# Two-layer decoder trunk on one core: retention scores of both heads in turn, regrouped retention outputs, and the first down-projection operands prepared and evicted on VectorE

## The chip, the cores and the metric

The kernel runs on one core of one Trainium2 chip. A core has TensorE (matrix products; the profile calls its products PE and its weight loads PEld), VectorE (DVE), ScalarE (ACT), GpSimd (POOL) and the queue of SyncE (SP) that issues the transfers. The metric is the device time of one execution, in microseconds (us); lower is better.

## The reference, cut to what matters

Each of two layers normalizes the 1024 x 1024 input, projects it into twelve slices of 256 columns, feeds four groups (a 31-tap convolution module, stick-breaking attention, chunkwise retention, a short gated convolution), projects their concatenation back, and then runs a gated convolutional feed-forward block. The change touches retention and the start of the feed-forward block's last product. Retention, for four heads of 64 columns and eight chunks of 128 positions:

```python
    def step(state, inp):
        qc, kc, vc = inp
        inner = jnp.einsum('bhqd,bhkd->bhqk', qc, kc) * d_intra
        o = jnp.einsum('bhqk,bhkd->bhqd', inner, vc) + jnp.einsum('bhqd,bhde->bhqe', qc, state) * q_decay[..., None]
        state = state * chunk_decay[:, None, None] + jnp.einsum('bhkd,bhke->bhde', kc * k_decay[..., None], vc)
        return state, o
...
def conv_ffn(x, w_up, w_conv, w_down):
    h = causal_dwconv(x @ w_up, w_conv)
    gate, up = jnp.split(h, 2, axis=-1)
    return (jax.nn.silu(gate) * up) @ w_down
```

## The kernel before

All large products are made in three passes: every operand is split into a rounded high part and a low part (`split`, L180 to L182: a ScalarE copy for the high part, then a VectorE subtraction for the low part), and high x high, high x low and low x high are added up in PSUM.

**The mixer of a layer.** Twenty-four column blocks of the input projection are computed one after another (`project`, L210, products of 128 x 128 by 512 columns). Between the eight inner steps of each block a slot counter advances (`run_slot`, L590), and each slot runs what is due in it: attention score units, retention steps, and the taps of the 31-tap convolution (L261, VectorE), which are put behind other work by a low priority. TensorE's order in this region is exactly the order of the program text; the other engines' orders are set by priorities. Retention runs twice per layer, for head pair 0 (from slot 94) and head pair 1 (from slot 160); its steps come at the offsets in `RET_AT`, 0, 6, 9, 12, 14, 17 and 18 for the part that matters here:

- offset 0: products for the states (L465 to L467), then the state recurrence on VectorE (L474 to L479);
- offsets 6 and 9: the scores of head 0 over all eight chunks, then of head 1 (L490 to L492, 24 products each). The two heads of a pair lie in the lower and upper 64 rows of the key tiles kh and kl and of the query tiles q2, so each product uses 64 of the 128 rows. `bank()` gives the PSUM tile. VectorE masks the result (L494), and `split` makes the high and low halves `it`;
- offsets 12, 14, 17, 18: the outputs, for each head and each half of four chunks (L510 and L512). For each chunk there is one product over all 128 rows (values with `it`), and, except for the very first chunk, one over the head's 64 rows (state with query), added to the same place. ScalarE and VectorE evict the result (L514 to L516).

**The feed-forward block.** The last gate and up products (`ffn_products`, L894) leave TensorE through the PSUM tiles x, y and z; the last eviction of x is the copy L948 on ScalarE. The down projection then takes over the same PSUM space (L1050). Its 22 column blocks are added up in ten chunks; for each chunk and each of eight row blocks `down_tok` (L982) makes 12 products (L977) into one of three rotating PSUM tiles. In the first chunk the result is copied to an SBUF tile by ScalarE (L987), in later chunks it is added by VectorE (L989). The operands of block j, the weights and the gated activations gd, come through `down_split` (L958): a transfer into a raw tile (L961), a ScalarE cast for the high part (L966), a subtraction for the low part (L967, on GpSimd or VectorE), and only then is the raw tile free again. Blocks 0 to 3 are loaded while the last `ffn_products` is still running (`freed`, L1028).

## Time and profile before

| what | value |
|---|---|
| median of three runs | 2420.81 us (2415.92 to 2422.47) |
| the profiled execution | 2420.78 us, of which its span is 2419.0 us |
| PE, PEld busy | 2329.3 us (96%), 1901.0 us (79%) |
| DVE, ACT, POOL busy | 1652.4 us (68%), 1094.2 us (45%), 239.4 us (10%) |
| mean granted TensorE clock | 0.985 |

A share of busy time is an average over stages. TensorE is busy nearly everywhere, and the change is worth what it is worth in the few stretches that it touches, so those are what the rows below are taken from. In a timeline row the bracket holds the idle time before the instruction and what ended it. In the chain of waits a step's length is the time from the end of the step before, so for products that follow each other it is the pace, while a timeline row's own length includes the overlap with its neighbours.

### The profile page before, as it was taken

How to read it: one execution, taken by the hardware profiler on the slowest of the kernel's cores; microseconds unless marked ns; L12 is line 12 of the kernel's file. 1: busy time of each engine (PE TensorE's matmuls, PEld its weight loads, DVE VectorE, ACT ScalarE, POOL GpSimd, SP SyncE). 2: the span in 40 equal slices, each digit the busy share in tenths (PEclk: the TensorE clock that was granted, in tenths of full speed). 3: DMA queues.
4: the chain of work that ended last, by engine and by line, in shares of the span. 5: the costliest groups of instructions: out<-in, count | busy, mean ns of one | idle time of the engine just before them, and what ended most of it. 6: DMA issues, size and time to landing. Idle time of an engine off the chain costs nothing.

```text
span 2419.0 us, 26348 instructions
## 1 busy us (share of the span) xinstructions
PE 2329.3 (96%) x10596; PEld 1901.0 (79%) x10596; DVE 1652.4 (68%) x1717; ACT 1094.2 (45%) x1479; POOL 239.4 (10%) x100
## 2 busy tenths in 40 slices
PE   7998999999999999999999989999999999989998
PEld 6877787777888887888778767878888888877886
DVE  4699875549777777344557997765597777763445
ACT  5653564434444455421347535653345544453102
POOL 0000000000000002743210000000000000045420
PEclk9998999999999999999999989999999999999999
DMA  4212212412222224422222122123122222224223
GB/s 148 70 53 62 61 36 71 146 54 87 70 88 87 79 79 148 175 86 88 96 70 70 53 62 54 34 96 131 53 87 79 86 89 88 79 104 174 87 70 122
DMA packets 58811, 209.88 MB, mean 87 GB/s; under 512 B 7104, under 2 KB 7872, under 8 KB 58688
## 3 DMA queue, kind: packets, MB, share of 16 engines
q1 hardware_dynamic: 58688, 208.19, 26.0%
q8 instruction: 83, 1.36, 0.2%
q14 instruction: 40, 0.33, 0.0%
HBM read 159.93 MB, written 39.85 MB: 83 GB/s over the span
## 4 chain that ended last, share of the span: by engine, by line
PE 37%; DVE 7%; ACT 3%; DMA 2%; issue 1%; POOL 0%; DVEq 0%; SPq 0%; POOLq 0%; ACTq 0%
PE pp L210 10%; PE pp L977 9%; PE ppx L894 8%; PE ppy L894 4%; DVE u L261 2%; PE ppz L894 2%; PE pp L731 1%; DVE u L182 1%; ACT u L151 1%; PE op L409 1%; DVE u L379 1%; DVE u L167 1%; DMA u<-gd 0%; PE tp L396 0%; DMA wr<-in_w_out 0%
## 5 line engine op out<-in xcount | busy, mean ns | idle before, releaser
L261 DVE SCALAR_TENSOR_TENSOR u<-u,par,u 128x1023 f32<-128x1023 f32 (+10 forms) x280 | 363.8, 1310 | 45.2 <-ACT u L786 40.9
L989 DVE TENSOR_TENSOR u<-u,pp 128x1024 f32<-128x1024 f32 x143 | 174.5, 1221 | 234.7 <-PE pp L977 234.6
L210 PE MATMUL pp<-hH,wh 128*128 128x512 f32 x960 | 327.0, 411 | 0.7 <-DVE u L182 0.5
L210 PE MATMUL pp<-hL,wh 128*128 128x512 f32 x960 | 313.0, 397 | 0.0
L967 POOL TENSOR_TENSOR u<-u,u 128x1024 fp32r<-128x1024 f32 x48 | 119.6, 2507 | 1937.9 <-DVE u L940 1853.0
L210 PE MATMUL pp<-hH,wl 128*128 128x512 f32 x960 | 311.1, 395 | 0.0
L977 PE MATMUL pp<-u,u 128*128 128x512 f32 x1152 | 268.9, 394 | 14.3 <-ACT u L948 8.5
L977 PEld LDWEIGHTS pp<-u,u 128*128 128x128 f32 x1152 | 217.4, 190 | 62.8 <-ACT u L948 9.4
L210 PEld LDWEIGHTS pp<-hL,wh 128*128 128x128 f32 x960 | 183.5, 191 | 40.4
L210 PEld LDWEIGHTS pp<-hH,wl 128*128 128x128 f32 x960 | 183.1, 191 | 40.5
L210 PEld LDWEIGHTS pp<-hH,wh 128*128 128x128 f32 x960 | 172.2, 192 | 37.0 <-issue 5.5
L731 PE MATMUL pp<-u,hH 128*128 128x512 f32 x512 | 140.2, 392 | 0.2
L977 PE MATMUL pp<-hH 128*128 128x512 f32 x576 | 131.5, 389 | 0.0
L977 PEld LDWEIGHTS pp<-hH 128*128 128x128 f32 x576 | 108.1, 188 | 22.4
L786 ACT ACTIVATE u<-u,par 128x1024 f32<-128x1024 f32 x76 | 87.7, 1155 | 73.7 <-DVE u L940 66.5
L894 PE MATMUL ppx<-u,wh 128*128 128x512 f32 x384 | 118.7, 390 | 1.8 <-ACT u L935 1.5
L966 ACT CAST u<-u 128x1024 fp32r<-128x1024 f32 x48 | 50.2, 1052 | 136.7 <-DMA u<-in_w_down 87.8
L731 PEld LDWEIGHTS pp<-u,hH 128*128 128x128 f32 x512 | 95.0, 188 | 20.2 <-ACT u L181 1.0
L195 DVE TENSOR_TENSOR wl<-wr,wh 128x1024 fp32r<-128x1024 f32 x60 | 73.6, 1227 | 51.6 <-ACT wh L193 51.4
L894 PE MATMUL ppx<-u,hH 128*128 128x512 f32 x352 | 108.4, 389 | 0.0
L193 ACT CAST wh<-wr 128x1024 fp32r<-128x1024 f32 x60 | 62.9, 1049 | 70.9 <-PE pp L210 56.3
L379 DVE TENSOR_TENSOR_SCAN u<-pp,u 128x1023 f32<-128x1023 f32 (+3 forms) x64 | 87.7, 1401 | 0.7
(243 smaller groups left out, 4457.2 us busy)
## 6 DMA issues: line engine op xcount, KB each, us to landing
wr<-in_w_up SPq DMA_DIRECT2D x50, 512.0 KB, 3.5
wr<-in_w_in SPq DMA_DIRECT2D x48, 512.0 KB, 3.6
gd<-u SPq DMA_DIRECT2D x44, 512.0 KB, 2.9
u<-in_w_down SPq DMA_DIRECT2D x44, 512.0 KB, 4.8
u<-gd SPq DMA_DIRECT2D x44, 512.0 KB, 4.1
u<-in_w_up SPq DMA_DIRECT2D x38, 512.0 KB, 4.3
xs<-u SPq DMA_DIRECT2D x24, 512.0 KB, 2.6
u<-xs SPq DMA_DIRECT2D x24, 512.0 KB, 3.6
```

Of the source, the lines that this page charges most:

```text
L193: nc.scalar.copy(wh, raw)
L195: eng.tensor_sub(wl, raw, wh.bitcast(F32))
L210: nc.tensor.matmul(ps[:, half * 512:(half + 1) * 512], w[:, kt, :], m[:, 4 * half:4 * half + 4, kt, :], start=(kt == 0 and m is hH and w i ...
L261: eng.scalar_tensor_tensor(acc[:, lo:hi], src[:, lo - s:hi - s], wc, acc[:, lo:hi], ALU.mult, ALU.add)
L379: nc.vector.tensor_tensor_scan(rev, z[:, o + 1:e + 1][:, ::-1], rev, r[:, e:e + 1], ALU.add, ALU.add)
L731: nc.tensor.matmul(ps[:, hs], a[:, t, k, :], w[:, hs], start=(k == 0 and a is hH and w is wo[k][0]), stop=(k == KT - 1 and a is hL))
L786: nc.scalar.activation(acc, ps, AF.Copy, scale=par[:, w + 2:w + 3])
L894: nc.tensor.matmul(ps, a[:, kt, :], x(m, kt), start=start and kt == 0 and a is wh and m == 0, stop=kt == 3 and a is wl, skip_group_check=True)
L966: nc.scalar.copy(h, raw)
L967: (nc.gpsimd if n is not None or len(slot_of) % 2 else nc.vector).tensor_sub(lo, raw, h.bitcast(F32))
L977: nc.tensor.matmul(ps[:, hs], a[:, ts_], w[:, hs], start=(i == 0 and w is h and a is gh), stop=(i == len(gs) - 1 and a is gl))
L989: nc.vector.tensor_add(facc[t], facc[t], ps)
```

## The change

The change has four parts.

1. The two score steps no longer belong to one head each. Each now covers one half of the chunks (four of eight) and both heads, and the products alternate between head 0 (lower 64 rows) and head 1 (upper 64 rows). Within one PSUM tile the two heads lie in different banks.
2. An output group issues its four 128-row products first and its three or four 64-row products after them, instead of in turn.
3. In `down_split`, the subtraction for the first four blocks of a layer (eight tiles) is on VectorE; for all later ones on GpSimd. Before, the tiles of those first blocks went to GpSimd or VectorE by the parity of the number of tiles in use.
4. The eviction of the first chunk in `down_tok` is on VectorE, with a raised priority, instead of on ScalarE.

```diff
@@ retention
-        its = []
-        for hh in range(2):
-            rows = slice(HD * hh, HD * hh + HD)
-            ip = ptile(bank(), (P, NB, P))
-            for c in range(NB):
+        its = [[], []]
+        for half in range(2):
+
+            ip = ptile(bank(), (P, 2, 4, P))
+            for j in range(4):
+                c = 4 * half + j
                 cs = slice(c * P, (c + 1) * P)
-                nc.tensor.matmul(ip[:, c, :], kh[rows, cs], q2[c // 4][rows, c % 4, 0], start=True, stop=False)
-                nc.tensor.matmul(ip[:, c, :], kh[rows, cs], q2[c // 4][rows, c % 4, 1], start=False, stop=False)
-                nc.tensor.matmul(ip[:, c, :], kl[rows, cs], q2[c // 4][rows, c % 4, 0], start=False, stop=True)
-            m = ualloc(F32, (P, NB, P))
-            nc.vector.tensor_mul(m, ip, tri.unsqueeze(1).broadcast_to([P, NB, P]))
-            it = [ualloc(F32R, (P, 4, 2, P)) for _ in range(2)]
-            for half in range(2):
-                split(it[half][:, :, 0, :], it[half][:, :, 1, :], m[:, 4 * half:4 * half + 4, :])
+                for a, part in ((kh, 0), (kh, 1), (kl, 0)):
+                    for hh in range(2):
+                        rows = slice(HD * hh, HD * hh + HD)
+                        nc.tensor.matmul(ip[:, hh, j, :], a[rows, cs], q2[half][rows, j, part],
+                                         start=(a is kh and part == 0), stop=(a is kl))
+            m = ualloc(F32, (P, 2, 4, P))
+            nc.vector.tensor_mul(m, ip, tri.unsqueeze(1).unsqueeze(1).broadcast_to([P, 2, 4, P]))
+            for hh in range(2):
+                it = ualloc(F32R, (P, 4, 2, P))
+                split(it[:, :, 0, :], it[:, :, 1, :], m[:, hh])
+                its[hh].append(it)
             ufree(m)
-            its.append(it)
-            if hh == 1:
+            if half == 1:
                 ufree(kh, kl)
             yield
...
                 for j in range(4):
                     c = 4 * half + j
-                    nc.tensor.matmul(op[:, j], value_block(v2, c, hh), it[half][:, j], start=True, stop=(c == 0))
+                    nc.tensor.matmul(op[:, j], value_block(v2, c, hh), it[half][:, j], start=(j % 2 == 0),
+                                     stop=False, skip_group_check=True)
+                for j in range(4):
+                    c = 4 * half + j
                     if c:
-                        nc.tensor.matmul(op[:, j], st[rows, c - 1, :], q2[half][rows, j], start=False, stop=True)
+                        nc.tensor.matmul(op[:, j], st[rows, c - 1, :], q2[half][rows, j], start=False,
+                                         stop=(j % 2 == 1), skip_group_check=True)
@@ down_split
-            (nc.gpsimd if n is not None or len(slot_of) % 2 else nc.vector).tensor_sub(lo, raw, h.bitcast(F32))
+            (nc.gpsimd if len(loads) >= 4 else nc.vector).tensor_sub(lo, raw, h.bitcast(F32))
@@ down_tok
             if first:
                 facc[t] = ualloc()
-                nc.scalar.copy(facc[t], ps)
+                with tc.high_priority(offset=HPE):
+                    nc.vector.tensor_copy(facc[t], ps)
```

Outside the places shown here the engines' orders are the same as before, in particular VectorE's order in the mixer.

The first place is TensorE, the last retention output group of layer 1, head pair 1. In a row the PSUM tile stands left of the arrow, then the moving and the stationary operand: u_696 is `it`, u_682 the values, u_684 the queries, u_688 the states. Before, and after:

```order
L510 MATMUL pp_278_11256<-u_696_11119,u_682_10847 128x256
L512 MATMUL pp_278_11256<-u_684_10865,u_688_10914 128x256
L510 MATMUL pp_278_11256<-u_696_11119,u_682_10847 128x256
L512 MATMUL pp_278_11256<-u_684_10865,u_688_10914 128x256
L510 MATMUL pp_278_11256<-u_696_11119,u_682_10847 128x256
L512 MATMUL pp_278_11256<-u_684_10865,u_688_10914 128x256
```

```order
L513 MATMUL pp_278_11256<-u_696_11121,u_682_10847 128x256 x4
L518 MATMUL pp_278_11256<-u_684_10865,u_688_10914 128x256 x4
```

Eight products that took turns between the two kinds are now two runs of four.

The second place is VectorE at the start of the down projection of layer 1: L930, L936 and L940 evict and add the last gate and up products, L261 are the taps of the last block, L989 is the first addition of the second chunk. Before:

```order
L795 TENSOR_TENSOR u_935_14876<-u_935_14876,u_937_14902 128x1024
L930 TENSOR_TENSOR u_946_14926<-u_944_14924,ppz_350_14923 128x512
L936 TENSOR_TENSOR u_947_14927<-u_945_14925 128x512
L940 TENSOR_TENSOR u_946_14926<-u_944_14924,ppy_349_14922 128x512
L261 SCALAR_TENSOR_TENSOR u_966_15043<-u_946_14926,par,u_966_15043 128x1023
```

After (L937, L943 and L947 are the old L930, L936 and L940; L974 is the moved subtraction, L995 the moved eviction):

```order
L974 TENSOR_TENSOR u_953_14962<-u_951_14959,u_952_14961 128x1024
L937 TENSOR_TENSOR u_946_14926<-u_944_14924,ppz_350_14923 128x512
L974 TENSOR_TENSOR u_959_14987<-u_957_14984,u_958_14986 128x1024
L943 TENSOR_TENSOR u_947_14927<-u_945_14925 128x512
L947 TENSOR_TENSOR u_946_14926<-u_944_14924,ppy_349_14922 128x512
L974 TENSOR_TENSOR u_950_14956<-u_948_14953,u_949_14955 128x1024
L974 TENSOR_TENSOR u_965_15025<-u_963_15022,u_964_15024 128x1024
L261 SCALAR_TENSOR_TENSOR u_966_15043<-u_946_14926,par,u_966_15043 128x1023
L974 TENSOR_TENSOR u_956_14981<-u_954_14978,u_955_14980 128x1024
L261 SCALAR_TENSOR_TENSOR u_966_15043<-u_946_14926,par,u_966_15043 128x1022
L995 COPY u_968_15086<-pp_351_15073 128x1024
```

The subtractions now stand among the evictions of the last products, and the copies of the first chunk follow them on the same engine.

The third place is ScalarE at the same time, between the eviction L935 and the last eviction of the x tile (L948, after the change L955). Before:

```order
L935 COPY u_945_14925<-ppx_348_14921 128x512
L966 CAST u_949_14955<-u_948_14953 128x1024
L966 CAST u_955_14980<-u_954_14978 128x1024
L966 CAST u_964_15024<-u_963_15022 128x1024
L786 ACTIVATE u_966_15043<-u_946_14926,par 128x1024
L948 COPY u_947_14927<-ppx_348_14921 128x512
```

```order
L942 COPY u_945_14925<-ppx_348_14921 128x512
L973 CAST u_949_14955<-u_948_14953 128x1024
L973 CAST u_964_15024<-u_963_15022 128x1024
L793 ACTIVATE u_966_15043<-u_946_14926,par 128x1024
L973 CAST u_955_14980<-u_954_14978 128x1024
L955 COPY u_947_14927<-ppx_348_14921 128x512
```

The same three casts and the same activation stand ahead of that eviction, with one cast now behind the activation.

## Rows read from the trace of the kernel before

**Rows 1.** The page, part 1: busy time, share of the span, instructions.

```profile
PE 2329.3 (96%) x10596; PEld 1901.0 (79%) x10596; DVE 1652.4 (68%) x1717; ACT 1094.2 (45%) x1479; POOL 239.4 (10%) x100
```

**Rows 2.** Busy time by stretch; columns PE, PEld, DVE, ACT, POOL, PEclk, DMA, GB/s.

```profile
262.00:340.00 78.00, 77.85 (x399) 64.25 (x398) 58.72 (x68) 52.31 (x67) 0.00 (x0) 1.00 0.15 41
969.60:973.00 3.40, 3.40 (x10) 2.63 (x8) 1.50 (x1) 2.89 (x3) 3.40 (x2) 0.50 0.00 0
1399.00:1433.40 34.40, 28.80 (x133) 23.08 (x131) 33.64 (x49) 11.08 (x18) 0.00 (x0) 0.90 0.34 92
1570.00:1615.00 45.00, 45.00 (x191) 32.53 (x191) 22.52 (x29) 20.41 (x24) 0.00 (x0) 0.96 0.24 80
```

**Rows 3.** The chain of waits, layer 1 (head pair 1, down projection): start, step, what.

```profile
1563.31 0.95 PE op L409 x8
...
1572.30 0.11 PE pp L491
...
1594.74 0.11 PE pp L510
1594.85 0.31 PE pp L512
...
1596.72 0.31 PE pp L512
...
2195.01 212.51 PE pp L977 x936
```

**Rows 4.** The same chain, layer 1, head pair 0, half clock.

```profile
1410.96 0.21 PE pp L492
...
1433.87 0.51 PE pp L512
1434.38 0.51 PE pp L510
```

**Rows 5.** What TensorE waited for from 1399 to 1462 us: total, times, longest.

```profile
PE pp L510 <- DVE u L379: 4.3, 1, 4.3
PE pp L510 <- DVE u L516: 3.5, 1, 3.5
```

**Rows 6.** Timelines of VectorE and TensorE, layer 1, head pair 0, first output group.

```profile
1423.40 1.23 DVE L329 SCALAR_TENSOR_TENSOR u<-pp,u 64x1024 fp32r<-64x1024 f32 x1
...
1425.08 0.40 PE L510 MATMUL pp<-u,u 128*128 128x256 f32 x2
```

**Rows 7.** What TensorE waited for from 940 to 1005 us (layer 0).

```profile
PE pp L977 <- ACT u L948: 3.3, 1, 3.3
PE pp L977 <- ACT u L987: 0.5, 1, 0.5
```

**Rows 8.** The same from 2130 to 2205 us (layer 1).

```profile
PE pp L977 <- ACT u L948: 5.2, 1, 5.2
PE pp L977 <- ACT u L987: 3.8, 3, 1.5
```

**Rows 9.** Timelines of ScalarE, GpSimd and VectorE, start of layer 1's down projection.

```profile
2154.34 1.05 ACT L966 CAST u<-u 128x1024 fp32r<-128x1024 f32 x1 [6.36 <-DMA u<-gd]
...
2160.64 1.99 ACT L966 CAST u<-u 128x1024 fp32r<-128x1024 f32 x2 [3.83 <-POOL u L967]
...
2163.59 0.56 ACT L948 COPY u<-ppx 128x512 f32<-128x512 f32 x1
...
2155.46 5.15 POOL L967 TENSOR_TENSOR u<-u,u 128x1024 fp32r<-128x1024 f32 x2 [5.33 <-ACT u L966]
...
2155.90 2.50 DVE L936 TENSOR_TENSOR u<-u 128x512 f32<-128x512 f32 x1 [5.70 <-ACT u L935]
2158.32 0.68 DVE L940 TENSOR_TENSOR u<-u,ppy 128x512 f32<-128x512 f32 x1
```

**Rows 10.** The page, part 5: a VectorE and a GpSimd subtraction; idle time before them.

```profile
L967 POOL TENSOR_TENSOR u<-u,u 128x1024 fp32r<-128x1024 f32 x48 | 119.6, 2507 | 1937.9 <-DVE u L940 1853.0
...
L195 DVE TENSOR_TENSOR wl<-wr,wh 128x1024 fp32r<-128x1024 f32 x60 | 73.6, 1227 | 51.6 <-ACT wh L193 51.4
```

## The prediction

> **What bounds the kernel now.** The page comes first: TensorE is busy for 2329.3 of 2419.0 us, no other engine for more than 68% [rows 1]. A shorter product therefore shortens the kernel, but only where TensorE is not already waiting, so I read each stretch that the change touches by itself [rows 2]. During the second retention pass of a layer (head pair 1, 1570 to 1615 us in layer 1) TensorE is busy for 45.00 of 45.00 us and VectorE for half of that: here a saved TensorE microsecond is a saved microsecond. During the first half of head pair 0 (1399 to 1433 us) it is the other way round: VectorE works for 33.64 of 34.40 us, and TensorE has 5.6 us to spare. From 262 to 340 us in layer 0, after head pair 0, TensorE is busy for 77.85 of 78.00 us again. Then I read what TensorE waits for. In head pair 0 it waits twice for VectorE before output products, 3.5 and 4.3 us [rows 5]. At the start of the down projection it waits for ScalarE: 3.3 + 0.5 us in layer 0 [rows 7], 5.2 + 3.8 us in layer 1 [rows 8]. Last, the pace of products that follow each other, as steps of the chain [rows 3].
>
> **Part 2, the regrouped outputs.** Eight attention products of one shape (128 rows, 256 columns) take 0.95 us, 0.12 each. In an output group the same size takes 0.11 for the first product and then 0.31 at every further step, because each one goes from 128 rows to 64 or back [rows 3]. So a change of shape costs 0.31 - 0.12 = 0.19 us. A group of eight has seven such changes inside, a group of seven (first half, no state for chunk 0) five; the return to the projection comes on top both times. After the change each has one. That saves 6 x 0.19 = 1.15 and 4 x 0.19 = 0.76 us. One head pair has two groups of each kind: 3.8 us. At head pair 1 all of it lies on TensorE's path: 2 layers x 3.8 = **7.6 us**.
>
> At head pair 0 the first group is worth nothing. It starts at 1425.08, right behind a VectorE eviction (L329) that runs from 1423.40 to 1424.63 [rows 6] in a queue without a gap, and the group behind it waits 3.5 us for L516 of the same queue. From that group on VectorE waits for TensorE's outputs, and a shorter group is passed on. These groups run mostly at half the granted clock, where a change of shape makes a step 0.51 us against 0.21 for a step that stays in one shape [rows 4] (the 0.21 is a score product's): 6 x 0.30 = 1.8 for the second group, 4 x 0.30 = 1.2 for the third, and 1.15 (layer 0, full clock) or 1.8 for the fourth. That is 4.15 + 4.8 = 8.95 us in the two layers. I keep two thirds, **6 us**, because the wait of 4.3 us for L379 moves only as far as its own chain through ScalarE and VectorE does; the bounds are 2.4 (only the last group counts, at full clock) and 9.
>
> **Part 1, the scores.** A score product takes a step of 0.11 us [rows 3], 24 make 2.7 us. The multiplications and splits on VectorE and ScalarE keep their number, size and place. No row shows two heads alternating, so the step is bounded from both sides. If the products of the two heads run beside each other, 24 take 12 steps, 1.35 us less. If each has to wait for the other as now, nothing is saved. If going from the lower to the upper 64 rows costs what a change of shape costs, each takes 0.31 and a group loses 24 x 0.2 = 4.8 us. I take a gain of 1.2: both heads use products of the same shape, so the nearest row is the step that stays in one shape, not the one that changes it, and the two heads have different rows and different PSUM banks. At head pair 1 that is 2 groups x 2 layers x 1.2 = **4.8 us**. At head pair 0 it is nothing: the queue that has no gap there is VectorE's.
>
> The Trainium skill's page "TensorEngine Tiling (Array Packing)", section "Key Properties", says that only changing the tiling mode drains the engine and that different tiles load weights and multiply in parallel; by it the gain is 1.35 per group, 5.4 us in all, and the sum would be 0.6 us lower. No row of before shows it.
>
> **Parts 3 and 4, the start of the down projection.** In layer 1, TensorE's first down product waits 5.2 us for the eviction L948, which ScalarE starts at 2163.59 and ends at 2164.15 [rows 8, 9]; so the gate and up products were over at 2158.95. Ahead of L948 in ScalarE's queue stand casts that wait until 2160.64 for GpSimd, which works off two subtractions in 5.15 us [rows 9]. On VectorE a subtraction takes 1.23 instead of 2.51 us [rows 10], and its neighbours lose a brake: the 512-column addition L936 took 2.50 us beside a busy GpSimd, L940 of the same width 0.68 [rows 9]. With a subtraction ahead of them (its cast ends at 2155.4, so until 2156.6), L936 and L940 end near 2158.0 instead of 2159.0. Then ScalarE has an activation (the 0.96 us between its casts' end and L948), a cast of 1.05 and L948 itself with 0.56: 2160.6. The wait falls from 5.2 to 1.7: 3.5 us. In layer 0, with 3.3 us of wait and the same queue, I take 2.3. The copies L987 (0.5 + 3.8 us of waits) leave a queue of casts that wait for transfers; VectorE needs 1.2 us for each and a row block takes 12 products of 0.227 (212.51 us for 936 [rows 3]), 2.7 us, so with three PSUM tiles they are covered even behind one tap and one subtraction: 4.3 us gone. Together 10.1 us; the bounds are 4.3 - 2 = 2 (the eviction as late as now, some copies late) and 12.8 (all waits gone). The wait in layer 0 is followed by 3.4 us of half clock with ten products, where 15 would fit [rows 2]: 1.1 us. If that goes in both layers it is 2.2 more; I count 0.7 and keep the rest for the range. The sum for these parts is **10.8 us**.
>
> What is queued behind the moved work: VectorE's taps of the last block, which nobody on TensorE needs before the last chunk. GpSimd loses 16 of its subtractions and is not waited for later.
>
> **The sum.** 7.6 + 6 + 4.8 + 10.8 = 29.2 us. The profiled execution took 2420.8 (2419.0 of span and 1.8 around it), the same as the median, so the forecast is 2391.6, **2392 us**. Its own range is 2384 to 2400.
>
> **Rivals.**
> *Loads one after another.* The score step of 0.11 us is as long for 128 columns as the 0.12 step for 256 [rows 3]; so it isn't the multiplication that sets it. If it is the weight load and loads never overlap, alternating heads gains nothing: 2391.6 + 4.8 = 2396 us. The Trainium skill's page "TensorE: Matmul & The Clock Gate", section "LDWEIGHTS (loading the stationary operand)", says that a load's time goes by its columns, not its rows, which fits this; the same page lets a load overlap a product of other rows.
> *The wait moves to VectorE.* Subtractions now stand between the evictions L930, L936 and L940 in VectorE's queue. A subtraction waits for its cast, a cast for its transfer, and one cast waited 6.36 us for one [rows 9]. If L940, and behind it L948, come as late as now, only the copies' 4.3 us less a little are saved: 2391.6 + 8 = 2400 us. Against it: that cast ended at 2155.4, early enough.
> *Alternating heads costs, slower.* If going to the other head's rows costs 0.2 us at full clock, as a change of shape does, head pair 1 loses 4 x 4.8 = 19 us and head pair 0, after its 3.8 us of spare time a layer, 2 x (9.6 - 3.8) = 12. Against the other 24.4 us that is about 2427 us, slower than before, and more where the half clock lasts longer. It decides from about 0.17 us per alternation, (24.4 + 7.6) / 192.
>
> **How the numbers follow.** The forecast has 0.66, the loads one after another 0.15, the wait on VectorE 0.12, the costly alternation 0.07 (the shape stays the same, which speaks against it). The first three end more than 0.3% below 2420.8, that is below 2413.5; 0.3% is about what a measurement of this kernel can tell from no change. With small parts of each for something unseen: faster 0.91, within 0.3% 0.04, slower 0.05. The range for 8 in 10 takes in the second and third case and the bounds of head pair 0 and of the half clock: 2383 to 2405 us.
>
> **What would show it.** Score products of head pair 1 at steps near 0.06 (right), 0.11 (rival 1) or 0.3 (rival 3); an output group of eight in about 1.2 us instead of 2.3; head pair 0 with the same end of its first output group as before; TensorE's wait for the eviction after the last gate and up product below 2 us, and no wait for the first chunk's copies. Wrong would be the forecast if TensorE waited longer for VectorE at the scores or outputs of head pair 1, or if VectorE's idle time at the start of the down projection ended on transfers.

## The result, and the profile after

The changed kernel takes 2386.25 us (median of four runs, 2384.02 to 2386.96) beside 2420.36 for the kernel before: a ratio of 0.9862 (95% interval 0.9849 to 0.9875), 34 us less (30 to 37). A second set of runs, the repeat further below, gave 0.9847 (0.9832 to 0.9862). Two executions of the experiments, one of `o_heads` (3838 us) and one of `best` (2566 us), ran at a lower granted clock (0.56 and 0.85) and are left out of the times below. The forecast was 2392, its range 2383 to 2405: right in direction and range, 6 us too high. The profiled execution took 2386.67 us, 2384.9 of it its span.

The page of the changed kernel, part 1, answers to [rows 1]: TensorE is busy for 32.0 us less, GpSimd for 43, VectorE for 22 more.

```profile
PE 2297.3 (96%) x10596; PEld 1885.0 (79%) x10596; DVE 1674.2 (70%) x1749; ACT 1080.7 (45%) x1463; POOL 196.5 (8%) x84
```

In the changed kernel the lines have moved: L494 is every score product, L513 the 128-row and L518 the 64-row output products, L901 the gate and up products, L955 the last eviction of x, L973 and L974 cast and subtraction of `down_split`, L984 the down products, L995 the first chunk's evictions. The chain of waits (start, step, what) at head pair 1 of layer 1 answers to [rows 3]: 24 score products take 1.49 us, 0.062 a step instead of 0.11, and an output group of eight is 0.47 + 0.66 us with one change of shape inside.

```profile
1561.72 1.49 PE pp L494 x24
...
1574.90 0.47 PE pp L513 x4
1575.37 0.66 PE pp L518 x4
```

What TensorE waited for in the whole run (total, times, longest), some rows: the waits of head pair 0 for VectorE (L379, L329, L523) answer to [rows 5]. The kernel before has, in its whole run, 8.6 us for L379 as well and these two:

```profile
PE pp L510 <- DVE u L516: 5.7, 2, 3.5
PE pp L510 <- DVE u L329: 1.1, 1, 1.1
```

In the changed kernel the wait for L379 is as long as before; that for L329, ahead of the first output product, has grown from 1.1 to 7.5 us, since TensorE comes to it earlier, and that for the addition L523 (L516 before) has fallen from 5.7 to 4.9.

```profile
PE pp L513 <- DVE u L379: 8.6, 2, 4.3
PE pp L513 <- DVE u L329: 7.5, 2, 3.8
...
PE ppx L901 <- DVE u L261: 5.7, 1, 5.7
PE pp L513 <- DVE u L523: 4.9, 2, 3.0
PE pp L984 <- ACT u L955: 4.6, 2, 3.0
```

The same view of two stretches, the start of the down projection in layer 0 and in layer 1, answers to [rows 7] and [rows 8]. The copies' waits are gone in both layers; the wait for the last x went from 5.2 to 1.5 us in layer 1 and hardly moved in layer 0.

```profile
PE pp L984 <- ACT u L955: 3.0, 1, 3.0
```

```profile
PE pp L984 <- ACT u L955: 1.5, 1, 1.5
```

Where the time went, from the starts of the same products in the timelines of the two profiled executions (us):

| product | before | after | shift |
|---|---|---|---|
| layer 0: first score product, head pair 0 | 209.41 | 208.13 | -1.3 |
| first score product, head pair 1 | 371.02 | 366.56 | -4.5 |
| product behind the last output group | 407.89 | 396.79 | -11.1 |
| first gate and up product of the last stage | 599.24 | 588.96 | -10.3 |
| last gate and up product ends | 964.80 | 953.73 | -11.1 |
| layer 1: first score product, head pair 0 | 1407.77 | 1398.04 | -9.7 |
| first score product, head pair 1 | 1571.97 | 1557.23 | -14.7 |
| product behind the last output group | 1610.40 | 1587.47 | -22.9 |
| last gate and up product ends | 2158.98 | 2134.86 | -24.1 |
| end of the span | 2419.0 | 2384.9 | -34.1 |

The first 1.3 us lie ahead of every changed instruction. Between the end of layer 0's down projection (1222.2 before, 1210.0 after, a shift of -12.2) and layer 1's first score product 2.5 us are lost, where nothing was changed: that much a single trace leaves open. The mean granted clock there (from 973 to 1408 us) is 1.00 before; the changed kernel's trace has two short falls in it, 0.65 from 1217.0 to 1220.5 us and 0.69 from 1326.5 to 1330.0.

### The profile page after: what moved, and what is told of

It reads as the page before. It is cut to its first block, busy times and chain, and to the rows that moved or that the text cites. A ratio compares the mean times of both kernels' runs of the same rounds, so it can differ in the third digit from the quotient of the medians.

```text
span 2384.9 us, 26334 instructions
## 1 busy us (share of the span) xinstructions
PE 2297.3 (96%) x10596; PEld 1885.0 (79%) x10596; DVE 1674.2 (70%) x1749; ACT 1080.7 (45%) x1463; POOL 196.5 (8%) x84
## 4 chain that ended last, share of the span: by engine, by line
PE 38%; DVE 7%; ACT 3%; DMA 1%; issue 1%; DVEq 0%; SPq 0%
PE pp L984 10%; PE pp L210 9%; PE ppx L901 8%; PE ppy L901 4%; DVE u L261 2%; PE ppz L901 2%; PE pp L738 1%; DVE u L182 1%; ACT u L151 1%; DMA wr<-in_w_out 1%; PE op L409 1%; DVE u L379 1%; DVE u L167 1%; PE tp L396 0%; DMA wr<-in_w_up 0%
## 5 line engine op out<-in xcount | busy, mean ns | idle before, releaser
L261 DVE SCALAR_TENSOR_TENSOR u<-u,par,u 128x1023 f32<-128x1023 f32 (+10 forms) x280 | 356.3, 1284 | 28.6 <-ACT u L793 24.4
L984 PE MATMUL pp<-u,u 128*128 128x512 f32 x1152 | 266.0, 392 | 6.1 <-ACT u L955 4.6
L984 PEld LDWEIGHTS pp<-u,u 128*128 128x128 f32 x1152 | 216.6, 189 | 52.4 <-ACT u L955 5.4
L974 POOL TENSOR_TENSOR hH<-u,hH 128x1024 fp32r<-128x1024 f32 x24 | 58.1, 2451 | 1946.5 <-ACT hH L973 1946.5
L984 PE MATMUL pp<-hH 128*128 128x512 f32 x576 | 131.5, 389 | 0.0
L984 PEld LDWEIGHTS pp<-hH 128*128 128x128 f32 x576 | 108.1, 188 | 22.4
L901 PE MATMUL ppx<-u,wh 128*128 128x512 f32 x384 | 118.4, 389 | 0.3 <-ACT u L926 0.3
L973 ACT CAST u<-u 128x1024 fp32r<-128x1024 f32 x48 | 50.2, 1052 | 128.9 <-DMA u<-in_w_down 85.7
L901 PE MATMUL ppx<-u,hH 128*128 128x512 f32 x352 | 108.4, 389 | 0.0
L379 DVE TENSOR_TENSOR_SCAN u<-pp,u 128x1023 f32<-128x1023 f32 (+3 forms) x64 | 87.8, 1403 | 0.7
```

The costliest lines, as they stand in the source:

```text
L261: eng.scalar_tensor_tensor(acc[:, lo:hi], src[:, lo - s:hi - s], wc, acc[:, lo:hi], ALU.mult, ALU.add)
L379: nc.vector.tensor_tensor_scan(rev, z[:, o + 1:e + 1][:, ::-1], rev, r[:, e:e + 1], ALU.add, ALU.add)
L901: nc.tensor.matmul(ps, a[:, kt, :], x(m, kt), start=start and kt == 0 and a is wh and m == 0, stop=kt == 3 and a is wl, skip_group_check=True)
L973: nc.scalar.copy(h, raw)
L974: (nc.gpsimd if len(loads) >= 4 else nc.vector).tensor_sub(lo, raw, h.bitcast(F32))
L984: nc.tensor.matmul(ps[:, hs], a[:, ts_], w[:, hs], start=(i == 0 and w is h and a is gh), stop=(i == len(gs) - 1 and a is gl))
```

## The experiments

**One part at a time.** Each kernel is the kernel before with one or two parts of the change; the diffs are those of the section on the change, so only the part is named.

Part 1 alone.

> The kernel before with part 1 alone (scores of both heads in turn). Theory: a group of 24 score products passes in 1.5 us instead of 2.8, and this counts at head pair 1 alone, where TensorE has no idle time: 4 groups x 1.33 = 5.3 us, so about 2415 beside 2420.4. At head pair 0 the groups get shorter too, but the output products behind them wait the longer for VectorE: nothing. Rival 1: head pair 0 counts as well, 8 x 1.33 = 10.6 us, 2410. Rival 2: the alternation gains only together with part 2: within 1 us of before.

Measured: 2409.9 us, ratio 0.9962 (0.9950 to 0.9974) to 2418.8, so 9.2 us less (6.3 to 12.1). From the first score product of head pair 1 to the product behind its last output group it takes 34.15 us in both layers, the kernel before 36.87 and 38.43. The first difference is 2.7 = 2 x 1.33, as expected; the second has another 1.6 in it, which is half clock (a granted clock of 0.50, the 1.2 GHz level). Rows of the windows view (columns as in [rows 2]) just behind the second score group of head pair 1, of the kernel before and of the changed kernel, show it:

```profile
1580.60:1584.00 3.40, 3.40 (x8) 2.45 (x8) 2.66 (x5) 1.14 (x2) 0.00 (x0) 0.50 0.49 154
```

```profile
1563.20:1566.60 3.40, 3.40 (x13) 2.12 (x12) 2.26 (x3) 2.09 (x3) 0.00 (x0) 1.00 0.03 6
```

TensorE never rested there, yet behind the second group of 24 score products of one head the granted clock fell to 0.50. In the five profiled kernels with the old scores (ten such stretches, two layers each) there are eight such windows, in seven of the ten; in the nine with both heads in one group (eighteen stretches) none. Why the clock falls there is not shown. At head pair 0 the trace gains 1.3 and 2.6 us over the two layers' stretches (first score product of head pair 0 to that of head pair 1), not nothing. But in the four profiled kernels whose code for it is that of before, this stretch takes 161.6 to 163.3 us in layer 0 and 161.8 to 164.2 in layer 1, so a gain of this size is not clear of the difference between executions. The first output product starts where it did, 17.0 us behind the first score product, so what is gained comes later; in layer 1 the mean granted clock of the stretch is 0.94 instead of 0.92, in layer 0 0.94 as before. The wait of the first output product takes the rest; it was 1.1 us in all in the kernel before:

```profile
PE pp L513 <- DVE u L329: 6.3, 2, 3.8
```

Rival 2 is out. By time, the 5.3 us of the theory lie outside the interval and the 10.6 of rival 1 inside it; by the trace part 1 is worth 5.3 us at head pair 1, 1.6 of clock there, and some 2 to 4 at head pair 0.

Part 2 alone.

> The kernel before with part 2 alone (output products regrouped, scores as before). Theory: at head pair 1 a group of eight passes in 1.23 instead of 2.40 us and one of seven in 1.11 instead of 1.88, (1.17 + 0.77) x 2 groups x 2 layers = 7.8 us; at head pair 0 the gain of the first group is lost in a wait for VectorE and the others give about 7: 15 us, so about 2405. Rival: head pair 0 stays with VectorE all the way and gives nothing alone: 7.8 us, about 2413.

Measured: 2408.9 us, ratio 0.9957 (0.9945 to 0.9970), 10.4 us less (7.3 to 13.3), between the two expectations: the interval takes in the rival's 7.8 and not the theory's 15. The groups of head pair 1 are as expected (1.23 and 1.11 us), 7.8 us; but this execution has three windows of half clock behind score groups of head pair 1, the one before had one, and so it loses 3 us of it again. Head pair 0 gains 2.7 and 3.6 us by its stretches. Its waits have grown here too (L520 is the second addition of an output group, L516 in [rows 5], which has 5.7 us in the whole run of before):

```profile
PE pp L510 <- DVE u L520: 8.9, 2, 4.5
```

Parts 3 and 4 together.

> The kernel before with parts 3 and 4 alone (first subtractions and first evictions of the down projection on VectorE). Theory: layer 0 gives 1 us (only the copies' waits), layer 1 about 9 to 10 (3.5 of the wait for the last gate and up eviction, 3.8 of the copies' waits, the rest the half clock that followed): 10 to 11 us, about 2410. Rival: part of this came from parts 1 and 2, since they bring the stage forward against its transfers: then it is under 7 us, over 2413.

Measured: 2403.1 us, ratio 0.9941 (0.9928 to 0.9954), 14.3 us less (11.1 to 17.4). From the last gate and up product to the end, layer 1 gains 7.8 us in the trace (the wait for the last x falls to 2.1, the copies' waits go), and the two gate and up stages are 1.7 us shorter each; 1.5 us of that is a wait for L935 in the kernel before, which is gone. Layer 0 keeps its wait:

```profile
PE pp L977 <- ACT u L948: 2.9, 1, 2.9
```

The three kernels' gains, 9.2 + 10.4 + 14.3, make 33.9 us, and the whole change gives 33 to 37: the parts add up as far as their intervals of about 3 us either way can tell.

**Parts 3 and 4 apart.**

> The kernel before with part 3 alone (the first subtractions on VectorE, the first chunk's copies still on ScalarE). Theory: parts 3 and 4 need each other. The first down product of layer 1 starts 3.5 us earlier, but the copies stay in ScalarE's queue behind casts that wait for transfers, so their wait grows from 3.8 to about 7 us: under 1.5 us in all, 2419 or more. Rival: the parts add up, 3.5 us in layer 1 and about 1 of the half clock behind it: about 2416, with the copies' wait at 3.8 as before.

Measured: 2405.6 us, ratio 0.9950 (0.9938 to 0.9962), 12.1 us less (9.2 to 15.0). My theory fell, and the rival's reason too: the copies, although they are still on ScalarE, no longer keep TensorE waiting in layer 1, and do so for 1.5 us in layer 0. What TensorE waited for there, in layer 1 and in layer 0:

```profile
PE pp L977 <- ACT u L948: 3.9, 1, 3.9
```

```profile
PE pp L977 <- ACT u L948: 2.6, 1, 2.6
PE pp L977 <- ACT u L987: 1.5, 1, 1.5
```

ScalarE's timeline in layer 1, of the kernel before and then of this one, tells why for the first copies. Ahead of them stands the activation L786 of the last block. In the kernel before ScalarE stood idle for 3.73 us ahead of it, until a GpSimd subtraction ended; with VectorE's subtractions that is 0.57.

```profile
2170.82 1.15 ACT L786 ACTIVATE u<-u,par 128x1024 f32<-128x1024 f32 x1 [3.73 <-POOL u L967]
...
2174.23 2.85 ACT L987 COPY u<-pp 128x1024 f32<-128x1024 f32 x3
```

```profile
2162.20 1.15 ACT L786 ACTIVATE u<-u,par 128x1024 f32<-128x1024 f32 x1 [0.57 <-DVE u L967]
2163.25 1.91 ACT L987 COPY u<-pp 128x1024 f32<-128x1024 f32 x2
```

In the kernel before that is 1.0 of the 3.8 us, TensorE's wait at 2175.29. The other two waits, 1.5 us at 2185.26 and 1.3 at 2195.01, are for copies behind casts that wait for transfers, as the prediction said. But GpSimd is behind the first of these too: no transfer was issued between 2155.07 and 2176.49, when a subtraction freed the raw tile, and that one (L967 into hL) stood behind others in GpSimd's queue. TensorE, ScalarE, GpSimd and SyncE (SPq) in the kernel before:

```profile
2175.29 8.48 PE L977 MATMUL pp<-u,u 128*128 128x512 f32 x36 [1.02 <-ACT u L987]
2185.26 5.05 PE L977 MATMUL pp<-u,u 128*128 128x512 f32 x21 [1.49 <-ACT u L987]
...
2183.25 1.05 ACT L966 CAST hH<-u 128x1024 fp32r<-128x1024 f32 x1 [6.17 <-DMA u<-in_w_down]
2184.20 1.00 ACT L987 COPY u<-pp 128x1024 f32<-128x1024 f32 x1
...
2161.77 9.02 POOL L967 TENSOR_TENSOR u<-u,u 128x1024 fp32r<-128x1024 f32 x3 [1.15 <-ACT u L966]
2173.11 3.35 POOL L967 TENSOR_TENSOR hL<-u,hL 128x1024 fp32r<-128x1024 f32 x1
...
2155.07 0.38 SPq L961 DMA_DIRECT2D u<-in_w_down  x1
2176.49 0.32 SPq L961 DMA_DIRECT2D u<-gd  x1
```

With part 3 alone the same subtraction ends at 2164.42 and the transfer goes out at 2164.45, 7.9 us behind the first down product's start instead of 12.3.

> The kernel before with part 4 alone (the first chunk's evictions on VectorE, the subtractions where they were). With part 3 alone the copies on ScalarE no longer kept TensorE waiting in layer 1. So the new theory is that the copies were late because GpSimd released raw tiles late and with them transfers and casts, and that part 4 gains only what part 3 gains as well: the wait for the last gate and up eviction stays at 5.2 us in layer 1 and 3.3 in layer 0, the waits for the copies (3.8 and 0.5) go, 4 to 5 us in all with some of the half clock behind them, about 2415 beside 2419. The prediction's own view gives nearly the same time (4.3). What tells the two apart is the sum: by the new theory parts 3 and 4 overlap by about 4 us (part 3 alone 13.1, both 15.7, so part 4 alone more than 15.7 - 13.1 = 2.6); by the prediction they add up, and part 4 alone gives 2.6.

Measured: 2414.3 us, ratio 0.9983 (0.9973 to 0.9994), 4.1 us less (1.5 to 6.5); in the trace layer 1 gains 2.6 us behind the last gate and up product. The waits of layer 1:

```profile
PE pp L977 <- ACT u L948: 5.3, 1, 5.3
PE ppx L894 <- ACT u L935: 1.1, 1, 1.1
PE pp L977 <- DVE u L988: 1.0, 1, 1.0
```

Part 4 alone leaves the wait for the last x of layer 1 at 5.3 us and takes 2.8 of the copies' 3.8. Either part alone removes most of the copies' waits. How far the two gains overlap stays open: 12.1 + 4.1 beside 14.3 are within the intervals.

**How far TensorE looks for a free row half.** The changed kernel with another order of the score products at head pair 1:

```diff
+            seq = [(j, a, part, hh) for j in range(4) for a, part in ((kh, 0), (kh, 1), (kl, 0)) for hh in range(2)]
+            if p == 1:
+                seq.sort(key=lambda e: (e[3], e[0]) if L == 0 else (e[0], e[3]))
+            for j, a, part, hh in seq:
```

> The changed kernel, but with another order of the score products at head pair 1, the PSUM tile laid out as it is: in layer 0 twelve products of head 0, then twelve of head 1, in layer 1 three of a chunk's head 0, then three of its head 1. Theory (two products run beside each other only if neighbours use different row halves): 24 products in 2.7 to 2.8 us in layer 0, as before the change, and between 1.5 and 2.8 in layer 1. Rival (the new layout, with a head in its own PSUM banks, is what made the products faster): 1.5 us in both.

Measured, in a single run (2381.0 us), in layer 0 by the timeline of TensorE (24 products start at 366.84, the projection's next at 369.28, so 2.44 us) and in layer 1 by the chain of waits:

```profile
366.84 2.51 PE L494 MATMUL pp<-u,u 64*128 64x128 f32 x24
369.28 0.50 PE L210 MATMUL pp<-hH,wh 128*128 128x512 f32 x1
```

```profile
1551.09 1.49 PE pp L494 x24
```

The layout is not it: runs of twelve are much slower than strict turns (2.44 beside 1.49; 2.82 before). But the theory's number for them, 2.7 to 2.8, was too high, and neighbours are not needed: runs of three are as fast as strict turns. The single products' starts in the kept traces show how. In strict turns and in runs of three the 24 products start in twelve pairs, 0.11 us apart, the two of a pair within 0.01 us. In runs of twelve (layer 0, from 366.84) eight start singly, 0.11 us apart, then four pairs, each within 0.06 us, then eight singly. A trace row doesn't name the half of the rows that a product uses, but one half alone starts a product every 0.11 us, so the reading is that a pair is one product of each half: at the border the other half's first product starts beside the ninth of its run, ahead of three that come earlier in the program.

**The same with 256 columns.** The changed kernel with each output step of head pair 1 over two chunks and both heads, whose 64-row products take turns:

```diff
+        for pair in range(4 if p == 1 else 0):
+            half = pair // 2
+            op = ptile(bank(), (P, 2, 2, 2, P))
+            cs = [(2 * pair + i, 2 * (pair % 2) + i) for i in range(2)]
...
+            for i, (c, j) in enumerate(cs):
+                for hh in range(2):
+                    rows = slice(HD * hh, HD * hh + HD)
+                    if c:
+                        nc.tensor.matmul(op[:, hh, i], st[rows, c - 1, :], q2[half][rows, j], start=False,
+                                         stop=(i == 1), skip_group_check=True)
```

> The changed kernel with another grouping of the outputs at head pair 1: each of the four steps covers two chunks of both heads (eight evictions of 64 x 256 more on VectorE and four more on ScalarE per head pair) and lets the 64-row products of the two heads take turns, in different PSUM banks. They are 256 columns wide, the score products 128. Theory 1 (products of different row halves run beside each other whatever their width): four state products pass in 2 x 0.11 instead of 4 x 0.11 us, a group of eight in about 1.0 instead of 1.23. Theory 2 (only the loads overlap, the columns pass one by one): 1.23 as now. In time at most 2 x 7 x 0.11 = 1.5 us: 2385 to 2386.

Measured: 2382.5 us (three runs, 2379.9 to 2389.2), ratio 0.9856 (0.9833 to 0.9878), no difference from the changed kernel that time can tell. In the chain of waits (L512 and L518 are here the 128-row and 64-row products) four state products pass in 0.44 us instead of 0.66, 0.19 of it the change of shape, and a group of eight in 1.00 us from its start to the next product:

```profile
1566.49 0.47 PE pp L512 x4
1566.96 0.44 PE pp L518 x4
```

Theory 1 holds: the multiplications overlap as well, not the weight loads alone.

**Head pair 0.** The changed kernel with the last two output groups of head pair 0 later:

```diff
-RET_AT = (0, 6, 9, 12, 14, 17, 18, 23, 25), (0, 7, 9, 12, 14, 17, 18, 24, 26)
+RET_AT = (0, 6, 9, 12, 14, 18, 20, 23, 25), (0, 7, 9, 12, 14, 17, 18, 24, 26)
```

> The changed kernel with the last two output groups of head pair 0 one and two places later (offsets 18 and 20 instead of 17 and 18), where their PSUM tile is not the one that an attention score unit holds until VectorE's scan L379. In the changed kernel TensorE waits 4.3 us for that scan in each layer. Theory: both waits go, and nothing behind needs these outputs earlier: 8 us less, about 2378. Rival: VectorE is the bound of this stretch all the same, and the wait comes back at the next product that needs it (the mean of the outputs, the next attention unit): within 2 us of the changed kernel, 2385.

Measured: 2380.1 us, ratio 0.9841 (0.9826 to 0.9857), which overlaps both intervals of the changed kernel. It lies 6.2 and 3.6 us below the medians of the changed kernel's two sets, between the theory's 8 and the rival's 2, so time alone doesn't decide. The waits of the whole run:

```profile
PE pp L361 <- DVE u L379: 10.7, 8, 1.7
PE pp L513 <- DVE u L523: 6.0, 2, 4.5
...
PE pp L513 <- DVE u L329: 4.7, 2, 2.5
...
PE mu L530 <- DVE u L523: 3.6, 2, 1.8
```

The 8.6 us for L379 at the output products are gone, and come back as 3.4 more at the next attention unit (L361), 3.6 at the mean of the outputs (L530), 2.1 at their variance (L538) and 1.1 for L523, with 2.8 less for L329: 7.4 of the 8.6. By stretches the gain is 2 us in layer 0 and 0.4 to 2.6 in layer 1 (against the two profiled executions of the changed kernel). By the waits the rival is right in the main: most of what was saved is waited for again at VectorE's next results, so VectorE bounds this stretch, as the prediction read it.

**The wait that stayed.** Why does the first down product of layer 0 still wait 3.0 us? ScalarE's timeline of the changed kernel, layer 0, then two rows of layer 1:

```profile
951.90 1.05 ACT L973 CAST u<-u 128x1024 fp32r<-128x1024 f32 x1 [2.99 <-DMA u<-in_w_down]
953.17 1.05 ACT L973 CAST u<-u 128x1024 fp32r<-128x1024 f32 x1 [0.21 <-DMA u<-gd]
954.12 1.15 ACT L793 ACTIVATE u<-u,par 128x1024 f32<-128x1024 f32 x1
955.17 1.03 ACT L973 CAST u<-u 128x1024 fp32r<-128x1024 f32 x1
956.11 0.58 ACT L955 COPY u<-ppx 128x512 f32<-128x512 f32 x1
```

```profile
2131.58 1.06 ACT L973 CAST u<-u 128x1024 fp32r<-128x1024 f32 x1 [1.53 <-DMA u<-in_w_down]
...
2135.78 0.58 ACT L955 COPY u<-ppx 128x512 f32<-128x512 f32 x1
```

L955 stands behind three casts and an activation, 4.2 us from the first of them on, and the first waits for a transfer that lands 1.83 us before the last gate and up product ends in layer 0 (951.90 to 953.73) and 3.28 before it in layer 1 (2131.58 to 2134.86). The wait of the product is what remains of it. Why the transfer lands later against the products in layer 0 is not shown. A repeat of the changed kernel and three others:

> The changed kernel once more, beside the two that follow, on the same chip: 2385 to 2387, ratio 0.986 to the kernel before. In its trace the first down product waits 3.0 us in layer 0 and 1.5 to 2.5 in layer 1 (the wait of layer 1 has been 3.9, 2.1, 2.0, 1.9 and 2.5 in other kernels with the subtractions on VectorE, that of layer 0 2.6, 2.9, 2.0 and 3.1).

Measured: 2383.7 us, ratio 0.9847 (0.9832 to 0.9862); waits of 3.0 and 1.5 us.

The next kernel leaves ScalarE alone and moves the PSUM space. In the changed kernel the first of the three down tiles lies where the last block's x and y lay; an unused tile allocated ahead of it takes that place, and the first down tile gets the next.

```diff
         psum("pp")
+        ptile(rot[0] % 3)
```

> The changed kernel, with one PSUM tile of the down projection allocated ahead of the first and left unused for its first turn. The three rotating tiles then lie one place further: the first takes the space of z and of the other block's x, which is evicted long before, and the space of the last x, which L955 evicts, goes to the third tile. Theory (the rest of the prediction's miss: what the first down product waits for is only that its tile lies where the last x was; how late L955 is hangs on casts that wait for transfers): both waits go, 3.0 in layer 0 and about 2 in layer 1, with a us or two of half clock behind them, and the third row block (5.4 us later) finds its tile free: 5 to 6 us less than the changed kernel, about 2380. Rival (the operands of the first products are what is late, the cast and subtraction of blocks 0 and 1): the first products wait nearly as long for VectorE or ScalarE, within 1 us of the changed kernel.

Measured: 2383.7 us, ratio 0.9848 (0.9835 to 0.9861): nothing gained. Yet the waits for L955 are gone in both layers, and what layer 0 waits for at its start now is VectorE's eviction, 1.9 us in all. The gain was lost elsewhere: in the whole run the wait for L261 has doubled, and the timeline shows the new one at the first gate and up product of layer 1, whose x now lies where the last plain block's tile is still read.

```profile
PE ppx L901 <- DVE u L261: 11.4, 2, 5.7
```

```profile
1767.89 0.76 PE L901 MATMUL ppx<-hH,wh 128*128 128x512 f32 x1 [5.68 <-DVE u L261]
```

The theory held at its place and its sum failed, because shifting the three tiles also shifted a later stage that takes over their space.

> The changed kernel with three edits together: the shifted PSUM tiles of the down projection, the two later output groups of head pair 0 (offsets 18 and 20), and the state products of the two heads in turn at head pair 1. Theory (they lie in different stretches and add up): 5 to 6 + 4 to 5 + 1.5 = 10 to 12 us less than the changed kernel, 2374 to 2376, ratio 0.982 to the kernel before. Rival (the later output groups only move VectorE's backlog on): 2379, ratio 0.9835.

Measured: 2381.2 us, ratio 0.9836 (0.9823 to 0.9848), as the rival's number. Its trace has both causes in it: the same 5.7 us for L261 in layer 1, which the rival didn't have, and, as with the later output groups alone, longer waits of the next attention units for L379 (10.6 us instead of 7.3), which are the rival's reason.

The last kernel has unused tiles ahead at both changes of stage, in each layer as it needs it, so that the first x and y, and the first down tile, lie where the stage before was done early; the later output groups and the state products in turn are in it too:

```diff
             psum("xyz")
+            for s in (("x0", "y0"), ())[l]:
+                ptile(s, (P, 512))
...
         psum("pp")
+        for s in ((1, 0), (0,))[l]:
+            ptile(s)
```

> As the kernel named best (shifted PSUM tiles at the down projection, later output groups, state products of the heads in turn), but with tiles placed so that no stage starts in the space that the stage before evicts last, in both layers: also where the gate and up products take over from the plain blocks. There the kernel before and the changed kernel wait 5.7 us in layer 0 for a tap L261 that reads the last plain block's PSUM tile, and the shift in space and best brought the same 5.7 us into layer 1 (the two kernels lost 5.9 us there and gained nothing in all). Theory (a wait at a change of stage is a matter of where the tiles lie): no wait for L955 or for L261 in either layer; 5.7 us less than best in layer 1 and 5.7 less in layer 0 with some of the half clock behind it, 11 to 14 us: 2367 to 2370, ratio 0.978. Rival (the stages are held by VectorE's or the transfers' pace and the waits come back behind): 2378 or more.

Measured: 2366.7 us (2364.95 to 2369.18), ratio 0.9791 (0.9777 to 0.9804) to the kernel before, 51 us less, and clearly below the changed kernel. It differs from the kernel named best in its unused tiles alone and is faster than it by 14 us by the medians, 11 by the ratios, as expected (11 to 14). The page's busy line, and two of the longest waits that are left (L361 is the next attention unit, L536 an output product, L546 the second addition of an output group):

```profile
PE 2283.5 (97%) x10596; PEld 1873.1 (79%) x10596; DVE 1676.6 (71%) x1765; ACT 1080.7 (46%) x1471; POOL 196.4 (8%) x84
```

```profile
PE pp L361 <- DVE u L379: 10.1, 8, 1.7
PE pp L536 <- DVE u L546: 9.0, 2, 4.5
```

No wait for the last x (L955) or for the tap (L261) is left at a change of stage. The mean granted clock is 0.994 beside 0.985 before and 0.986 after: 2 x (1 - clock) x span gives some 28 us at half clock instead of 73 and 67 (the rounded clock leaves 2 us open). One of these stretches can be read: behind the 5.7 us wait for L261 in layer 0 the granted clock of the kernel before is 0.50 from 597.6 to 604.2 us, and where the last kernel starts the same products without a wait, from 578 to 590 us, it is 1.00.

## Why the prediction was right, point by point

**Part 2, head pair 1 (7.6 us).** Right: groups of eight went from 2.39 to 1.23 us and of seven from 1.88 to 1.11, (1.16 + 0.77) x 4 = 7.7. A change of shape costs 0.19 us at full clock for both sizes of group, so it is a price per change.

**Part 1, head pair 1 (4.8 us).** Right, a little small: 2.82 to 1.49, 4 x 1.33 = 5.3. The choice of the nearest row (a step within one shape) over the row for a change of shape was the right one. The Trainium skill, page "TensorEngine Tiling (Array Packing)", section "Key Properties", has different tiles load and multiply in parallel, by which 5.4 was worked out; this trace agrees, with 5.3. The rival of loads one after another and the costly alternation are both out. The price of the latter had a term that no row gives, 3.8 us of spare time a layer at head pair 0; [rows 2] leave 5.6 (34.40 - 28.80), with which it would be some 2424 us instead of 2427.

**Head pair 0 (6 us for part 2, 0 for part 1).** The reading held where it was most definite: the first output product starts with the same shift as the first score product, -1.3 us in layer 0 (226.42 to 225.14), so nothing that was saved up to there reaches it. The size was too small: the stretches got 3.2 and 5.0 us shorter, 8.2. By the kernels with one part each, the 6 for part 2 was near (2.7 + 3.6 = 6.3), and the step that failed is "At head pair 0 it is nothing" for part 1 (1.3 + 2.6 = 3.9). Shorter groups also change what falls into half clock, which the sum counted for part 2 and not for part 1. All of these are differences of single traces, in a stretch that varies by some 2 us by itself.

**The start of the down projection (10.8 us).** The sum was near, 1.2 in layer 0 (a shift of -11.1 becomes -12.2 at the end of the layer) and 10.0 in layer 1, but its split was wrong in two steps, so that the sum came out is in part luck. The step "in layer 0, with 3.3 us of wait and the same queue, I take 2.3" failed: 0.3 was gained. The queue is the same, but with GpSimd out of it the transfers decide, and in layer 0 they land later beside TensorE's last product. What was missing there came in layer 1, where the waits explain 7.5 of the 10.0 us; among the rest is the half clock behind the first down product (a granted clock of 0.51 from 2164.2 to 2167.6 us before; 1.00 from 2136.4 to 2145.0 after), for which 0.7 was counted. The step for layer 1, 5.2 to 1.7, came out at 1.5, but over all kernels with part 3 and the tiles in their old places the wait lies between 1.5 and 3.9, where with GpSimd it was 5.2 to 5.3 each time. It was read as a chain of fixed durations, and hangs on a landing. The prediction had named idle time of VectorE that ends on transfers as a sign against it; the sign showed on ScalarE. The other step is the copies: the 4.3 us were put to part 4, and part 3 alone removes the 3.8 of layer 1. The reason given, casts that wait for transfers, holds for 2.8 of them, but it left out what let the transfers start: after 2155.07 the next one was held by a GpSimd subtraction, as the activation ahead of the first copies was. With the subtractions off GpSimd the copies are in time on either engine.

One reading of [rows 9] needs care. L940 was set beside L936 as the addition without a brake, but by its row it ran from 2158.32 to 2159.00, while GpSimd was busy until 2160.61, and took 0.68 us all the same. The brake on L936 was there: in each of the four profiled kernels that have GpSimd's subtractions at this place, two of these 38 additions took 2.50 us, and in the changed kernel, where GpSimd does nothing there, all 38 (L943) took 0.69 or less. But L940 was never longer than 0.69 in any of the four. The two differ in their operands: L940 reads a PSUM tile and L936 none.

**What the sum left out.** It came to 29.2 us, the trace to 34.1. Beside head pair 0 (2.2 more) and part 1 at head pair 1 (0.5) there are the window of half clock behind the scores of head pair 1 in layer 1 (1.6), the gate and up stages (0.8 + 1.2 by the table, 1.5 of it the waits for L935), and 0.4 at the down projection; against that about 2 us of difference between executions. Two of these were visible in the trace of before, as a granted clock of 0.96 in [rows 2] and as a third wait, 1.1 us for L935, in the view of [rows 8].

## What to carry to other kernels

Order products so that those on different halves of the rows lie within a few places of each other, and those of one shape in one run; the first was worth 0.05 us a product and the second 0.19 a change here, and in full only where TensorE is what the stretch waits for. Where one stage takes over the PSUM space of another, look which tile of the old stage is read last and put the new stage's first tile elsewhere: that was 5.7 + 3.0 + 1.5 us of waits and some half clock behind them, with no instruction changed; and look at every later stage that inherits the places. The wait that varied here from kernel to kernel (1.5 to 3.9 us) hung on a transfer's landing: such a wait is better costed by its bounds than by a chain of durations. And where a wait ends on a transfer, ask what let the transfer start: here it was a GpSimd subtraction that freed the raw tile.

## What the runs showed of the hardware that was not expected

- TensorE needs no strict turns: 24 products of 64 rows in runs of three take the 1.49 us of strict turns, in runs of twelve 2.44, of one head alone 2.82. Their starts come in pairs, twelve pairs in runs of three and four at the border of runs of twelve. The half of the rows isn't marked in the trace; that a pair is one product of each half, started ahead of up to three earlier ones, is the reading.
- Products of 256 columns on different row halves overlap as those of 128 do: four in 0.44 us instead of 0.66, change of shape included.
- TensorE at work without a gap was granted half the clock behind 2.82 us of products that used 64 rows each, in seven of ten stretches; with both heads in one group, in none of eighteen. One such window cost 1.6 us (38.43 beside 36.87). The cause is not shown.
- A VectorE addition of 512 columns that reads no PSUM tile (L936) took 2.50 us beside a busy GpSimd, eight times in four kernels, and 0.68 without; one that reads a PSUM tile (L940) took 0.68 beside it too.
